# Two projections of a hybrid trunk layer by seven products in place of eight, and the last two groups of a third as one sum

## The chip, the cores and the metric

One core of a Trainium2 chip. The metric is device microseconds of one execution of the program; lower is better. The program holds two kernels one after the other: the fast one that is spoken of here, and a general one that runs only if the fast one, at its end, finds that some operand lay outside the range for which its number format holds.

## The reference

One layer for 1024 prompt tokens and 8 x 16 sample tokens (1152 columns in all), model width 1024:

```python
proj = h @ w_in                                   # q | k | v | SiLU gates | SSD x,B,C | dt | two merge gates
att_branch = (o_att.reshape(b, s, ATT_WIDTH) * jax.nn.silu(z_att)) @ w_att_proj    # 1024 -> 1024
...
y = rms_norm(y.reshape(b, s, SSD_GROUPS, SSD_WIDTH // SSD_GROUPS), ...)
ssd_branch = y.reshape(b, s, SSD_WIDTH) @ w_ssd_proj                               # 2048 -> 1024
merged = jax.nn.sigmoid(g_att) * att_branch + jax.nn.sigmoid(g_ssd) * ssd_branch
out = x + gate * (merged @ w_out)                                                  # 1024 -> 1024
```

The change touches the last three products: the attention projection, the SSD projection and the output projection.

## The kernel before

Activations lie transposed, 128 channels on the partitions and the 1152 tokens as columns. Every float32 operand of a large product is split into a float16 high part and a float16 low part, and a product is three matmuls: high x high, high x low, low x high (L709, L710, L712 in `dense`). The split of a tile is one ScalarE copy (the high part) and one VectorE instruction `x*scale - hi` (the low part): L627 and L628 in `halves` for weights, 1024 columns each, L1946 and L1948 in `split` for operands, 1152 columns each. `level` (L619) is a ScalarE square with a sum that records the mean size of what was split; `verdict` compares all of these with bounds at the end.

`dense` makes one tile of 128 output channels: for each of three groups of 384 tokens it sums over the 8 tiles of the operand, 3 matmuls each, in one PSUM bank (tag "d", three slots; "g" has three, "s" one of two banks). With `wide`, the three groups advance together, tile by tile, so that a first output tile can begin before the last operand tile is there.

The tail of the program is a row of stages on TensorE. First come the last of the gate products, which still use the 8 operand tiles of the input (`hops`). Then the attention projection, `att_dense`: 8 output tiles; each group's bank is read by one VectorE instruction that multiplies it with a gate tile (L1998). Then the SSD projection, `ssd_dense`, 4 groups of 4 operand tiles; for each group all 8 output tiles are made, and each bank is read by L2007 (times the gate) and added to the running sum by L2008. Then the output projection, `out_dense`, whose banks are read by L2070 (times the modulation, plus the residual), L2074 and L2076 for the samples, and stored. Beside these run the generators `att_prep` (loads the 8 attention tiles and starts their splits), `gate_loads`, `ssd_prep` (loads the SSD tiles, scales them by the norm, L1986, and starts their splits) and `mod_gate` (a small product for the modulation, within the attention projection).

The order of the instructions on each engine is not the order of the Python code: the class `Order` takes the recorded program, its dependencies and a table of costs, and lays every engine's instructions out by a list scheduler. Each engine then works through its own list strictly in that order, with semaphores between engines. Loads and stores of the tail are issued by SyncE's queue, in its own fixed order; among them are two short transfers, `ya` (L1133, stores three rows of token sums) and the load that brings them back (L1141), which belong to the norm of the last SSD group.

Of the kernel before, what the change touches and what calls it, by code (L numbers as in the profile page):

```python
# [64 lines left out]
X_MEAN = (0.25, 2.0 ** 19)  # L65

# [353 lines left out]
def trunk_kernel(ctx: ExitStack, tc: tile.TileContext, h, again):  # L420
# [42 lines left out]
    NPART, NOPER = 121, 48  # L463
    sums = fix(NPART + 2 + NOPER)
# [34 lines left out]
    L_TAIL = arena.set_layout(Z0, [("T", 15, NT)])  # L499
    L_SM = arena.set_layout(Z0 + 15 * NT, [("e", 2, 384)])  # L500
# [14 lines left out]
    def alloc(lay, tag, cols):  # L515
        if lay is L_H or lay is L_W or lay is L_W3 or lay is L_Q or lay is L_V:
            return Buf(arena, arena.alloc(lay, tag, cols // 2), cols, True)
# [83 lines left out]
    def job(*raw):  # L601
        jobs.append([len(parts) + i for i in range(len(raw))])
        parts.extend(raw)
# [9 lines left out]
    meant = {"w": 0, "x": NPART + 2}  # L613
# [15 lines left out]

    def w_split(i, keep=lambda x: x):  # L630

        n = len(jobs[i])
        w = parts[jobs[i][0]].shape[1]
        if i not in wsplit:
            lay = L_W3 if n > 1 else L_W
# [41 lines left out]
    def w_done(i):  # L677
        for x in wsplit.pop(i)[:2]:
            x.free()
# [10 lines left out]
    for x in [h["wall"][i] for i in range(29, 85)] + [h["watt"][i] for i in range(8)] + [h["wssd"][i] for i in range(16)] \  # L690
            + [h["wout"][i] for i in range(8)]:
        job(x)
# [1242 lines left out]
    gates = []  # L1935

# [5 lines left out]

    def split(t, ops, scale):
        hi = yield from walloc(L_H, "h", NT)
        lo = yield from walloc(L_H, "h", NT)
# [7 lines left out]

    att_ops, out_ops = [], []
    ssd_ops = [[] for _ in range(NG)]

    def att_prep():
        yield from ready(lambda: ssd_all[NPAIR])
        for u in range(NU):
            t = yield from walloc(L_TAIL, "T", NT)  # L1960
            dma(t.ap, att_d[u])
            yield from pause(3000)
            urgent.append(split(t, att_ops, SA))

    def gate_loads():
        yield from ready(lambda: len(att_ops) >= NU - 1)
        for i in range(16):
            t = yield from walloc(L_TAIL, "T", NT)
            dma(t.ap, gate_d[i])
            gates.append(t)  # L1970
            yield from pause(5000 if i < 2 else 10500)

    def ssd_prep(g):
        yield from ready(lambda: len(ssd_ops[g - 1]) == PPG if g else len(att_ops) == NU)
# [3 lines left out]
        for j in range(PPG + 1):  # L1978
# [5 lines left out]
            if j:  # L1984
# [4 lines left out]
                urgent.append(split(t, ssd_ops[g], SA))  # L1989

    def att_dense():
        for c in range(8):
            def ev(o, g, tok, ps, c=c):
                while len(gates) <= c:
                    blocked[0] = "gates"
                    yield None
                x = gates[c].ap[:, tok]
                nc.vector.scalar_tensor_tensor(x, x, 1.0, ps, ALU.add, ALU.mult)  # L1998
# [1968 lines left out]
```

## Time and profile before

| | us |
|---|---|
| median of 3 runs | 1764.83 (1762.36 to 1766.66) |
| the profiled execution | 1765.52 |
| its span | 1763.6 |
| TensorE busy | 1738.2 (99%) |
| VectorE busy | 1230.0 (70%) |
| ScalarE busy | 957.8 (54%) |
| GpSimd busy | 347.3 (20%) |
| granted TensorE clock, mean | 0.998 |

A matmul's duration in the profile is from its start until its result is out; matmuls overlap, so what counts is the time from one start to the next. Loads of weights ("PEld") are engine time of their own that overlaps the matmuls. Durations of VectorE and ScalarE include a small overlap with the next instruction.

### The profile page before, as it was taken

The numbers are of one execution on the slowest core, as the hardware profiler recorded it, in microseconds if no ns is written. First come the engines' busy times: TensorE is split into PE (matmuls) and PEld (weight loads), VectorE is DVE, ScalarE is ACT, GpSimd is POOL, SyncE is SP. The second block draws the span as 40 slices with busy tenths as digits, with TensorE's granted clock in tenths as the row PEclk, the third lists the DMA queues.
The fourth block names the chain that finished last, engine by engine and source line by source line (L and its number), as shares of the span: only waits on it lengthen the run. The fifth ranks groups of instructions, "written<-read, shape, count | busy, mean of one in ns | idle before, by whom it ended". The sixth has DMA issues, their size and how long they took to land.

```text
span 1763.6 us, 34941 instructions
## 1 busy us (share of the span) xinstructions
PE 1738.2 (99%) x13821; PEld 1092.9 (62%) x13821; DVE 1230.0 (70%) x2327; ACT 957.8 (54%) x1903; POOL 347.3 (20%) x624
## 2 busy tenths in 40 slices
PE   7999999999999999999999999999999999999998
PEld 3556556555556566666666666666666556666665
DVE  6458677877776967787878677777775526876732
ACT  8766555556465565656764656456552616342510
POOL 0233323323133011321312131112222100000000
PEclk9999999999999999999999999999999999999999
DMA  9248878988887584533554445435577734311321
GB/s 381 74 125 206 196 213 198 206 211 195 204 232 165 148 230 131 174 114 124 174 158 114 107 132 181 140 117 133 165 227 271 270 103 156 102 49 50 128 104 56
DMA packets 266565, 284.87 MB, mean 162 GB/s; under 512 B 199628, under 2 KB 200664, under 8 KB 266392
## 3 DMA queue, kind: packets, MB, share of 16 engines
q1 hardware_dynamic: 257432, 253.90, 51.9%
q0 software_dynamic: 8960, 28.65, 4.3%
q8 instruction: 110, 1.80, 0.4%
q14 instruction: 63, 0.52, 0.1%
HBM read 192.70 MB, written 43.66 MB: 134 GB/s over the span
## 4 chain that ended last, share of the span: by engine, by line
PE 87%; DVE 5%; ACT 4%; DMA 2%; issue 1%; POOL 1%; SPq 0%; DVEq 0%; POOLq 0%; ACTq 0%
PE d L709 19%; PE d L710 18%; PE d L712 18%; PE d L762 5%; PE d L764 5%; PE d L763 5%; PE g L1368 2%; PE s L1855 2%; PE g L1827 2%; PE g L1875 1%; PE s L1415 1%; PE g L1415 1%; PE g L712 1%; PE g L710 1%; PE g L709 1%
## 5 line engine op out<-in xcount | busy, mean ns | idle before, releaser
L709 PE MATMUL d<-arena 128*128 128x384 f16 x2172 | 709.6, 327 | 1.4 <-ACT arena L1543 1.4
L710 PE MATMUL d<-arena 128*128 128x384 f16 x2172 | 708.7, 326 | 0.0
L712 PE MATMUL d<-arena 128*128 128x384 f16 x2172 | 708.6, 326 | 0.0
L709 PEld LDWEIGHTS <-arena 128*128 128x128 f16 x2280 | 223.5, 98 | 147.8 <-issue 10.5
L712 PEld LDWEIGHTS <-arena 128*128 128x128 f16 x2280 | 223.2, 98 | 147.8 <-issue 0.5
L710 PEld LDWEIGHTS <-arena 128*128 128x128 f16 x2280 | 223.3, 98 | 138.0 <-issue 2.0
L619 ACT ACTIVATE arena<-arena 128x1024 bf16<-128x1024 f32 (+3 forms) x169 | 181.5, 1074 | 145.0 <-DMA arena<-in_wall_dram 82.4
L627 ACT ACTIVATE arena<-arena 128x1024 f16<-128x1024 f32 (+1 forms) x117 | 122.4, 1046 | 124.5 <-PE d L710 112.6
L762 PE MATMUL d<-arena 128*128 128x384 f16 (+1 forms) x568 | 186.8, 329 | 0.0
L764 PE MATMUL d<-arena 128*128 128x384 f16 (+1 forms) x568 | 186.1, 328 | 0.0
L763 PE MATMUL d<-arena 128*128 128x384 f16 (+1 forms) x568 | 186.1, 328 | 0.0
L628 DVE SCALAR_TENSOR_TENSOR arena<-arena 128x1024 f16<-128x1024 f32 (+1 forms) x117 | 145.3, 1246 | 42.3 <-ACT arena L627 41.7
L1308 ACT ACTIVATE arena<-arena 128x640 f32<-128x640 f32 (+4 forms) x144 | 100.8, 701 | 62.6 <-DVE arena L1311 62.1
L1566 DVE SCALAR_TENSOR_TENSOR arena<-arena 128x1176 f32<-128x1176 f32 x72 | 107.2, 1489 | 2.3 <-issue 0.9
L1754 ACT ACTIVATE arena<-arena 128x128 f32<-128x128 f32 x288 | 89.9, 390 | 28.0 <-DMA arena<-acs_d 26.3
L762 PEld LDWEIGHTS <-arena 128*128 128x128 f16 x576 | 56.3, 98 | 50.7 <-issue 17.5
L1344 DVE SCALAR_TENSOR_TENSOR arena<-arena 128x640 f16<-128x640 f32 (+4 forms) x128 | 86.9, 711 | 0.0
L1236 POOL TENSOR_SCALAR arena<-arena 128x16 f32<-128x16 f32 (+1 forms) x24 | 10.0, 415 | 356.3 <-DVE arena L1209 356.1
L764 PEld LDWEIGHTS <-arena 128*128 128x128 f16 x576 | 56.4, 98 | 38.4 <-issue 0.2
L1203 ACT ACTIVATE arena<-d 128x256 f32<-128x256 f32 x71 | 26.8, 378 | 96.1 <-PE d L764 96.1
L763 PEld LDWEIGHTS <-arena 128*128 128x128 f16 x576 | 56.4, 98 | 32.8
L1311 DVE CUSTOM_DVE_ANT_0 arena<-s,arena 128x320 f32<-128x320 f32 (+4 forms) x128 | 60.2, 502 | 19.4 <-PE s L1473 9.4
(242 smaller groups left out, 2596.4 us busy)
## 6 DMA issues: line engine op xcount, KB each, us to landing
arena<-in_wall_dram SPq DMA_DIRECT2D x85, 512.0 KB
arena<-acs_d SPq DMA_DIRECT2D x32, 576.0 KB
arena<-in_kc_dram SPq DMA_DIRECT2D x64, 256.0 KB
arena<-in_vc_dram SPq DMA_DIRECT2D x64, 256.0 KB
arena<-in_wada_dram SPq DMA_DIRECT2D x24, 512.0 KB
arena<-in_xT_dram SPq DMA_DIRECT2D x16, 576.0 KB
gate_d<-arena POOLq DMA_DIRECT2D x48, 192.0 KB, 4.0
arena<-eacs_d SPq DMA_DIRECT2D x32, 288.0 KB
```

What stands on the lines that cost most here:

```text
L619: keep(nc.scalar.activation(junk[:, :n], x, AF.Square, scale=scale * n ** -0.5, accum_out=sums[:, c:c + 1]))
L627: keep(nc.scalar.activation(hi, x, AF.Copy, scale=scale))
L628: keep(nc.vector.scalar_tensor_tensor(lo, x, scale, hi, ALU.mult, ALU.subtract))
L709: nc.tensor.matmul(ps, hi.r[:, wc], kh.r[:, tok], start=k == 0, stop=False)
L710: nc.tensor.matmul(ps, hi.r[:, wc], kl.r[:, tok], start=False, stop=False)
L712: nc.tensor.matmul(ps, lo.r[:, wc], kh.r[:, tok], start=False, stop=k == nk - 1)
L762: nc.tensor.matmul(ps, kh.r[:, tok], wh, start=k == 0, stop=False)
L763: nc.tensor.matmul(ps, kh.r[:, tok], wl, start=False, stop=False)
L764: nc.tensor.matmul(ps, kl.r[:, tok], wh, start=False, stop=k == KT - 1)
L1308: nc.scalar.activation(p, p, AF.Exp, bias=sm_[:, 4 + e:5 + e], scale=-1.0, accum_out=sm_[:, 6 + e:7 + e])
L1566: nc.vector.scalar_tensor_tensor(yc, r.ap[:, j:j + n], w4[:, i, j:j + 1], yc, ALU.mult, ALU.add)
L1754: nc.scalar.activation(me[e].ap[:, cs], me[e].ap[:, cs], AF.Relu, scale=-1.0, bias=a4[:, c, hds[e]:hds[e] + 1])
```

## The change

In `att_dense` and `out_dense`, two output tiles (256 channels) and the two halves of the tokens (576 each) form a 2 x 2 block product over pairs of operand tiles. The new `quad_dense` makes it by Strassen's scheme in Winograd's form: 7 products instead of 8, each over 4 pairs of operand tiles, in two banks of 288 tokens, 3 matmuls each. What the scheme adds:

- `quad_split` makes four sums of 512 columns of the two weight tiles and splits 3.5 tiles where 2 were split (each of 1024 columns).
- `pieces` takes two operand tiles, makes four sums of 576 columns, and splits 3.5 tiles of 1152 columns where 2 were split; `level` reads the four half tiles.
- `joined` (L795 of the changed kernel) adds a product's two banks to a running sum, seven times for each block product; the first product is copied out by ScalarE (L816; at the first block product of a stage a second one too, L820).

All of these sums are VectorE's. In `ssd_dense` groups 2 and 3 become one sum over 8 operand tiles, so that the banks are read for three groups, not for four. Sizes of pools, the loads' conditions and the bounds of `verdict` follow.

```diff
+    def quad_split(i):
...
+        a, b = ([x.ap.rearrange("p (k e m) -> p e k m", e=2, m=P)[:, e] for e in range(2)] for x in w)
...
+        halves(bufs[0].r, bufs[1].r, w[0].ap, SW)
+        nc.vector.tensor_tensor(t[0], b[0], b[1], ALU.add)
+        nc.vector.tensor_tensor(t[1], t[0], a[0], ALU.subtract)
+        nc.vector.tensor_tensor(t[2], a[0], b[0], ALU.subtract)
+        nc.vector.tensor_tensor(t[3], a[1], t[1], ALU.subtract)
...
+        halves(bufs[3].r, bufs[4].r, u[0].ap, SW)
+        halves(k4(bufs[2].r[:, :512]), k4(bufs[2].r[:, 512:]), b[1], SW)
+        halves(bufs[5].r, bufs[6].r, u[1].ap, SW)
...
+    HT = NT // 2
+    HC = NT // 4
+
+    def quad_dense(ops, evict, last=False, wide=False):
...
+        def product(q, banks, ks=range(4)):
...
+                for g, ps in enumerate(banks):
+                    c = slice(g * HC, (g + 1) * HC)
+                    nc.tensor.matmul(ps, wh, xh[:, c], start=k == 0, stop=False)
+                    nc.tensor.matmul(ps, wh, xl[:, c], start=False, stop=False)
+                    nc.tensor.matmul(ps, wl, xh[:, c], start=False, stop=k == 3)
...
+        def joined(t, banks, op):
+            y = yield from walloc(L_TAIL, "T", HT)
+            for g, ps in enumerate(banks):
+                c = slice(g * HC, (g + 1) * HC)
+                nc.vector.tensor_tensor(y.ap[:, c], t.ap[:, c], ps, op)
+            return y
+
+        def bank(n):
+            if n % 3 == 0:
+                x = pss.tile([P, 2, 512], F32, tag="s", name=nm("s"))
+                return [x[:, g, :HC] for g in range(2)]
+            if n % 3 == 1:
+                return [pg(HC) for _ in range(2)]
+            return [psd.tile([P, HC], F32, tag="d", name=nm("d")) for _ in range(2)]
...
+        if wide:
+            qs = (0, b), (1, bank(1)), (2, bank(2))
+            for k in range(4):
+                for q, x in qs:
+                    yield from product(q, x, (k,))
...
+        s1 = yield from walloc(L_TAIL, "T", HT)
+        for g, ps in enumerate(b):
+            nc.scalar.activation(s1.ap[:, g * HC:(g + 1) * HC], ps, AF.Copy)
...
+        yield from product(1, b)
+        c = yield from joined(s1, b, ALU.add)
+        yield from evict(0, 0, c) or ()
+        b = bank(2)
+        yield from product(5, b)
+        u2 = yield from joined(s1, b, ALU.add)
...
+        yield from product(6, b)
+        u3 = yield from joined(u2, b, ALU.add)
...
+        yield from product(4, b)
+        c = yield from joined(u3, b, ALU.add)
+        yield from evict(1, 1, c) or ()
+        u4 = yield from joined(u2, b, ALU.add)
...
+        yield from product(3, b)
+        c = yield from joined(u3, b, ALU.subtract)
+        yield from evict(1, 0, c) or ()
...
+            yield from product(2, b)
+        c = yield from joined(u4, b, ALU.add)
+        yield from evict(0, 1, c) or ()
...
+    def pieces(ta, tb, ops, scale):
...
+        got[0], = yield from halved(b11, HT)
+        got[1], got[2] = yield from halved(tb.ap[:, :NT], NT)
...
+        nc.vector.tensor_tensor(t1, b12, b11, ALU.subtract)
+        nc.vector.tensor_tensor(t2, b22, t1, ALU.subtract)
+        nc.vector.tensor_tensor(t3, b22, b12, ALU.subtract)
+        nc.vector.tensor_tensor(t4, t2, b21, ALU.subtract)
+        for x in (b11, b12, b21, b22):
+            level(x, scale, kind="h")
...
+        got[4], got[5] = yield from halved(u[0].ap[:, :NT], NT)
+        got[6], got[3] = yield from halved(u[1].ap[:, :NT], NT)
...
     def ssd_dense(g):
...
-            yield from dense(ssd_ops[g], ev, nk=4, outs=2, last=cp == 3, other=g < NG - 1)
+            yield from dense(ssd_ops[g], ev, nk=4 if g < NL else 8, outs=2, last=cp == 3, other=g < NL)
...
     def out_dense():
...
+            def ev(o, t, y, c=c, xs=xs):
...
+                nc.vector.scalar_tensor_tensor(x.ap[:, a:a + n], y.ap[:, :n], m[:, 0:1], x.ap[:, a:a + n], ALU.mult, ALU.add)
+                if t:
...
+                    nc.vector.tensor_tensor(y3, y3, m[:, 1:].unsqueeze(2).to_broadcast([P, NB, NS]), ALU.mult)
+                    nc.vector.tensor_tensor(x.ap[:, NP:], x.ap[:, NP:], y.ap[:, n:], ALU.add)
+                dma(h["out_y"][c + o][:, a:a + HT], x.ap[:, a:a + HT])
```

Since the scheduler lays the engines' lists out anew, three places are shown. The first is SyncE's queue around the token sums of the last SSD group, shortly before the attention projection. `att_d` is the attention's result, `ya` the row of sums. Before:

```order
L1981 DMA arena_73<-y_d_76 128x1152
L1969 DMA arena_73<-gate_d_79 128x1152
L2026 DMA arena_73<-in_wada2_dram 128x1024
L1981 DMA arena_73<-y_d_76 128x1152
L2026 DMA arena_73<-in_wada2_dram 128x1024
L609 DMA arena_73<-in_watt_dram 128x1024
L1969 DMA arena_73<-gate_d_79 128x1152
L1133 DMA ya692_15201<-arena_73 1x384 x3
L1969 DMA arena_73<-gate_d_79 128x1152
L1141 DMA arena_73<-ya692_15201 128x9
```

Now:

```order
L2204 DMA arena_73<-att_d_75 128x1152
L618 DMA arena_73<-in_watt_dram 128x1024
L2214 DMA arena_73<-gate_d_79 128x1152
L1296 DMA ya692_15231<-arena_73 1x384 x3
L2214 DMA arena_73<-gate_d_79 128x1152
L2276 DMA arena_73<-in_wada2_dram 128x1024
L1304 DMA arena_73<-ya692_15231 128x9
L2204 DMA arena_73<-att_d_75 128x1152
L2276 DMA arena_73<-in_wada2_dram 128x1024
```

Before, all eight loads of `att_d` stood ahead of `ya` (the last of them ahead of the rows shown); now the eighth stands behind both transfers of the token sums (L1296 and L1304 are the old L1133 and L1141).

The second is ScalarE's list at the entry of the attention projection. L1658 (now L1821) is the tanh that empties a bank of the last gate product. Before, L1946 is the high part of an operand and L619 a `level`:

```order
L1658 ACTIVATE arena<-d_15185 128x384
L619 ACTIVATE arena<-arena 128x1152
L1946 ACTIVATE arena<-arena 128x1152
L1658 ACTIVATE arena<-d_15186 128x384
L1658 ACTIVATE arena<-d_15187 128x384
L1946 ACTIVATE arena<-arena 128x1152
L619 ACTIVATE arena<-arena 128x1152 x3
L627 ACTIVATE arena<-arena 128x1024
```

Now L2165 is a high part in `pieces`, L628 a `level`, L636 a high part of weights, L816 and L820 the copies out of PSUM:

```order
L1821 ACTIVATE arena<-d_15215 128x384
L1821 ACTIVATE arena<-d_15216 128x384
L1821 ACTIVATE arena<-d_15217 128x384
L2165 ACTIVATE arena<-arena 128x576
L628 ACTIVATE arena<-arena 128x576 x4
L2165 ACTIVATE arena<-arena 128x1152 x2
L628 ACTIVATE arena<-arena 128x1024 x2
L816 ACTIVATE arena<-s_15353 128x288 x2
L636 ACTIVATE arena<-arena 128x1024
L820 ACTIVATE arena<-d_15356 128x288
L820 ACTIVATE arena<-d_15357 128x288
```

Behind the last tanh stood one high part of an operand; now three high parts and six `level`s stand between it and the four copies that empty banks.

The third is VectorE's list at the end of the program. Before, the last two banks are read by one instruction each:

```order
L2055 TENSOR_SCALAR arena_73<-g841_18278 128x48
L2076 TENSOR_TENSOR arena_73<-arena_73 128x128
L2056 SCALAR_TENSOR_TENSOR arena_73<-arena_73 128x48
L2057 TENSOR_REDUCE arena_73<-arena_73 128x1
L2060 TENSOR_SCALAR again_58<-g842_18285 1x1
L2070 SCALAR_TENSOR_TENSOR arena_73<-d843_18289,arena_73 128x384
L2070 SCALAR_TENSOR_TENSOR arena_73<-d844_18316,arena_73 128x384
```

Now (L2333, L2336 and L2337 are the old L2070, L2074 and L2076; L2319 is the old L2060):

```order
L795 TENSOR_TENSOR arena_73<-arena_73,d861_18717 128x288
L2316 TENSOR_REDUCE arena_73<-arena_73 128x1
L2333 SCALAR_TENSOR_TENSOR arena_73<-arena_73 128x576
L795 TENSOR_TENSOR arena_73<-arena_73,s862_18746 128x288
L2319 TENSOR_SCALAR again_58<-g859_18711 1x1
L795 TENSOR_TENSOR arena_73<-arena_73,s862_18746 128x288
L2333 SCALAR_TENSOR_TENSOR arena_73<-arena_73 128x448
L2336 TENSOR_TENSOR arena_73<-arena_73 128x128
L2337 TENSOR_TENSOR arena_73<-arena_73 128x128
```

Behind the last product stood one instruction; now six stand there, and the verdict's last step is among them.

More of the change, by code (lines that the diff above doesn't have):

```diff
@@ L677, in w_done @@
     def w_done(i):
-        for x in wsplit.pop(i)[:2]:
+        w = wsplit.pop(i)
+        for x in w[0] if i in quads else w[:2]:
             x.free()
@@ L1935, in trunk_kernel @@
     gates = []
+    gone = [0]
     def gates_dense():
@@ L1988, in ssd_prep, with ev @@
                     rb.free()
[L1989 removed]
+                urgent.append(split(t, ssd_ops[min(g, NL)], SA))
     def att_dense():
[L1992 to L1994 removed]
+        for c in range(0, 8, 2):
+            def ev(o, t, y, c=c):
+                while len(gates) <= c + o:
                     blocked[0] = "gates"
                     yield None
[L1997 to L2000 removed]
+                x = gates[c + o].ap[:, t * HT:(t + 1) * HT]
+                nc.vector.scalar_tensor_tensor(x, x, 1.0, y.ap, ALU.add, ALU.mult)
+                y.free()
+            yield from quad_dense(att_ops, ev, last=c == 6, wide=c == 0)
+            gone[0] = c + 2
     def ssd_dense(g):
```

262 lines of the change are left out of this document (211 added, 51 removed).

## The prediction

> **What bounds the kernel now.** First the page's head and the engines' totals:
>
> ```profile
> span 1763.6 us, 34941 instructions
> ...
> PE 1738.2 (99%) x13821; PEld 1092.9 (62%) x13821; DVE 1230.0 (70%) x2327; ACT 957.8 (54%) x1903; POOL 347.3 (20%) x624
> ```
>
> TensorE is busy 99% of the span, VectorE 70%. Then the tail by stages: the gate products, the attention projection, the SSD projection, the output projection, and what lies behind the last matmul (columns: TensorE, weight loads, VectorE, ScalarE, GpSimd busy, granted clock, DMA share, GB/s).
>
> ```profile
> 1310.00:1376.00 66.00, 66.00 (x471) 42.68 (x469) 36.44 (x49) 23.56 (x36) 17.70 (x26) 1.00 0.76 267
> 1376.00:1475.00 99.00, 99.00 (x626) 58.68 (x624) 39.01 (x52) 37.74 (x57) 4.61 (x12) 1.00 0.48 174
> 1475.00:1663.00 188.00, 188.00 (x1159) 113.20 (x1158) 147.72 (x231) 75.52 (x101) 0.00 (x0) 1.00 0.28 89
> 1663.00:1757.40 94.40, 94.30 (x582) 56.58 (x580) 32.28 (x62) 21.51 (x31) 0.00 (x0) 1.00 0.27 96
> 1757.40:1763.60 6.20, 0.00 (x0) 0.00 (x0) 0.56 (x1) 0.00 (x0) 0.00 (x0) 0.77 0.12 40
> ```
>
> TensorE never waits there. So a matmul taken from these stages is worth its pitch, as long as VectorE and ScalarE empty the banks in time. VectorE is used 39 of 99 us in the attention projection and 32 of 94 in the output projection, so that the added sums fall where it has room; in the SSD projection it works 148 of 188 us and TensorE still loses nothing.
>
> **The matmuls.** The pitch is read from starts, here of the last gate product; between the first and the last row lie 23 matmuls:
>
> ```profile
> 1374.22 0.33 PE L712 MATMUL d<-arena 128*128 128x384 f16 x1
> ...
> 1377.96 0.33 PE L710 MATMUL g<-arena 128*128 128x384 f16 x1
> ```
>
> 3.74/23 = 0.1626 us for 384 columns. Removed are 2 projections x 8 tiles x 8 operand tiles x 3 groups x 3 = 1152 of these, 187.3 us. Added are 8 block products x 7 x 4 x 2 banks x 3 = 1344 of 288 columns. None of that width is in the trace, so I bound it by neighbours: 416 columns in a dense product, and two widths of the attention scores, with the matmul behind each.
>
> ```profile
> 548.02 0.35 PE L762 MATMUL d<-arena 128*128 128x416 f16 x1
> ...
> 548.91 0.34 PE L764 MATMUL d<-arena 128*128 128x416 f16 x1
> 364.85 0.67 PE L1415 MATMUL s<-arena 64*128 64x128 f16 x12
> 365.45 0.34 PE L762 MATMUL d<-arena 128*128 128x384 f16 x1
> 370.65 0.82 PE L1415 MATMUL s<-arena 64*128 64x512 f16 x6
> 371.40 0.34 PE L762 MATMUL d<-arena 128*128 128x384 f16 x1
> L709 PEld LDWEIGHTS <-arena 128*128 128x128 f16 x2280 | 223.5, 98 | 147.8 <-issue 10.5
> ```
>
> 416 columns: 0.89/5 = 0.178, so in proportion to 384 (0.176) within the rounding of the starts; a line through 384 and 416 would give 0.116 at 288, a saving of 30.9 us, the far end below. The scores (half arrays, 128 columns in 0.60/12 = 0.050, 512 in 0.75/6 = 0.125) have a fixed part of 0.025; with that at full array 288 columns would be 0.025 + 0.1376 x 0.75 = 0.128, a saving of 187.3 - 172.3 = 15.0, the far end above. I take the proportion, 0.122, since 416 against 384 is the same form of matmul: 163.9 us, a saving of **23.4**. A weight load (98 ns) still fits beside 122.
>
> The Trainium skill (TensorE: Matmul & The Clock Gate, "Wait — 56ns, not 53.3ns?") speaks against this a little: warm matmuls start N/2.4 GHz plus a fixed 2.5 ns apart, and this change issues 192 more. By it 288 columns are 122.5 ns, and the saving 22.7 us in place of 23.4; the rows at 384 and 416 fit it as well as the proportion.
>
> **VectorE.** The durations:
>
> ```profile
> L628 DVE SCALAR_TENSOR_TENSOR arena<-arena 128x1024 f16<-128x1024 f32 x36 | 44.4, 1233 | 12.0 <-ACT arena L627 11.9
> L1948 DVE SCALAR_TENSOR_TENSOR arena<-arena 128x1152 f16<-128x1152 f32 x32 | 43.1, 1353 | 16.5 <-ACT arena L1946 16.3
> L1986 DVE SCALAR_TENSOR_TENSOR arena<-arena 128x1152 f32<-128x1152 f32 x16 | 22.6, 1415 | 9.4 <-DMA arena<-y_d 6.8 <-DMA arena<-yb 2.5
> L1621 DVE TENSOR_TENSOR arena<-g,arena 128x288 f32<-128x288 f32 x1 | 0.4, 440 | 0.0
> L1881 DVE TENSOR_TENSOR arena<-arena 128x512 f32<-128x512 f32 x16 | 11.0, 690 | 0.4
> L2007 DVE SCALAR_TENSOR_TENSOR arena<-arena,d 128x384 f32<-128x384 f32 x87 | 47.5, 550 | 25.5 <-PE d L712 25.5
> L2008 DVE TENSOR_TENSOR arena<-arena 128x384 f32<-128x384 f32 x96 | 52.2, 554 | 1.7
> ```
>
> For one block product: 14 joins x 0.44 = 6.2; 4 evictions of 576 columns at 0.76 (between 0.55 at 384 and 1.23 at 1024) = 3.0; the next weights 2 x 1.23 + 0.69 for 512 = 3.2 and four sums x 0.69 = 2.8. Together 15.2 us beside 168 x 0.122 = 20.5 of TensorE. The attention projection adds the first SSD operands (5 x 1.415 + 4 x 1.353), the first SSD weights and small things: 73 us beside 82 plus 5 of the modulation's matmuls, 84%. The output projection has about 70 beside 82. The operands of each projection cost 4 pairs x (0.76 + 3 x 1.35 + 4 x 0.76) = 31 us where 8 x 1.35 = 11 stood; for attention this lies beside the gate products (36 of 66 us used), for the output beside the SSD sum over 8 tiles, which in turn loses 24 x (0.550 + 0.554) = 26.5 us of bank reading. That fusion takes no matmul away and TensorE did not wait there, so it is worth **0** by itself, but it is the cover of the rest: the SSD stage then has 148 - 26.5 + 31 + 6 (the first output weights) = 158 us of VectorE work in 188, and without it 185, 98%.
>
> TensorE is ahead of VectorE by two products at most: the banks go s, g, d in turn, and a product lasts 2.9 us. I walked the second block product of the attention projection, with the modulation in it, through the new order: each bank was emptied before it was needed, by 0.5 us or more. A wait of 0.25 us at each of the 56 products would be 14 us, the far end; none is the near one, to which the walk is nearer. I take **1.0**.
>
> **The entry of the attention projection.** The rows on the eighth load and ScalarE:
>
> ```profile
> 1365.80 0.85 PE L1128 MATMUL g<-arena 128*32 128x384 f32 x6
> 1367.21 0.84 SPq L1133 DMA_DIRECT2D ya<-arena  x3
> 1370.37 0.34 SPq L1141 DMA_DIRECT2D arena<-ya  x1
> 1376.82 0.33 PE L709 MATMUL g<-arena 128*128 128x384 f16 x1
> y_d<-arena POOLq DMA_DIRECT2D x16, 576.0 KB, 4.5
> L1946 ACT ACTIVATE arena<-arena 128x1152 f16<-128x1152 f32 x32 | 36.0, 1152 | 34.1 <-PE g L712 16.3 <-DVE arena L2008 10.3 <-PE d L712 7.4
> L627 ACT ACTIVATE arena<-arena 128x1024 f16<-128x1024 f32 x113 | 118.9, 1052 | 124.5 <-PE d L710 112.6 <-PE g L710 11.6
> L619 ACT ACTIVATION_READ_ACCUMULATOR arena<-arena 128x1 f32 x169 | 32.0, 189 | 0.0
> L1614 ACT ACTIVATE arena<-g 128x288 f32<-128x288 f32 x1 | 0.4, 410 | 3.3 <-PE g L1613 3.3
> ```
>
> Call the projection's first matmul T (1376.82). The load behind L1141 goes out at T-6.0 and, by the 4.5 us that a transfer of this size takes, lands at T-1.5. What needs it late is the fourth pair: TensorE has 54 matmuls (6.6 us) before it. VectorE makes the three sums, the low part and the rest by about T+8.7, product 5 wants its piece at T+9.9. ScalarE is tighter: after the last tanh (T+0.7) come 0.65 (576 columns, between 0.41 at 288 and 1.15 at 1152), four `level`s (3.4, with 0.19 each for the read-out), two high parts (2.3), two `level`s of weights (2.5), so that the copies of the first bank end at T+10.3 and, after 1.05 and 0.41, the first of the other at T+11.8. TensorE wants these at T+10.2 and T+11.1: a stall of **1.0**, between 0 (pitches are some 0.1 under the durations) and 4.5 (one more landing).
>
> At the output projection the same walk from the last three SSD banks (six readings, three sums, two splits: about T+6.2 for the first pieces, wanted at T+6.6) gives nothing.
>
> **The end.**
>
> ```profile
> 1756.97 0.33 PE L712 MATMUL d<-arena 128*128 128x384 f16 x1
> 1757.34 0.62 DVE L2070 SCALAR_TENSOR_TENSOR arena<-d,arena 128x384 f32<-128x384 f32 x1 [3.28 <-PE d L712]
> 1757.98 0.33 SPq L2081 DMA_DIRECT2D out_y_dram<-arena  x1
> L2076 DVE TENSOR_TENSOR arena<-arena 128x128 f32<-128x128 f32 x8 | 2.3, 292 | 0.2
> ```
>
> One reading of 0.62 becomes 2 x 0.44, the verdict's last step (at most the 0.29 of 128 columns), 0.68 for 448 columns and 2 x 0.29: 2.4 us, all on the path; the last store is 288 KB, not 192. I take **+1.8**; the ends are 1.0 (the first bank read early) and 3.5 (the store held up by the register load, which now stands just ahead of it on SyncE).
>
> **Sum.** 1763.6 - 23.4 + 1.0 + 1.0 + 1.8 = 1744.0 for the span. The median lies 1.2 above this span (the profiled execution 1.9), so the forecast is **1745.2**.
>
> **Rivals.**
>
> VectorE becomes the bound. It works its list strictly in order, and behind each join stand weights and operands of the next block. If through such waits it gets only 75% of a stage, the projections last 73/0.75 = 97 and 70/0.75 = 94 us in place of 87 and 82: +22, so 1767; at 70% it is +35 and 1781. The gain is gone when the 56 products lose 0.35 us each. For it speaks the 84%; against it the SSD stage, 79% with TensorE at 188 of 188.
>
> The handovers are dearer: the eighth load lands 4.5 us later and the output's first pieces 3 us later, +7, so 1752. For it: the load's place behind two short transfers; against: 6.6 us of cover.
>
> The narrow matmul has the scores' fixed part: a saving of 15, so 1754. Against it stand the 416 columns.
>
> The change does not do what it says: the new bounds of the verdict fail, the general kernel runs too, and the time is beyond 3400 (at least the 1738 us of matmuls again). The halves' squares are compared within a factor of 64; the inputs make the cached values of the samples 7.56 times larger, in 128 of the 576 tokens of one half: (448 + 128 x 57)/576, a factor of some 13.
>
> **How the numbers follow.** The forecast (1741 to 1749) 0.62; dear handovers (1749 to 1758) 0.16; the fixed part 0.05; VectorE as the bound 0.16, of which 0.06 within 0.2% (3.5 us, about what a measurement of this kernel can tell from no change) and 0.10 above; the general kernel 0.01. So faster 0.83, same 0.06, slower 0.11. The range 1740 to 1758 holds the forecast, the fixed part and the dear handovers, 0.83; what it leaves out is VectorE as the bound and the general kernel.
>
> **What would show it.** Starts of 288-column matmuls 0.122 apart, and the span from the first of them in a projection to its last about 82 us (87 with the modulation); a wrong pitch shows there and nowhere else. TensorE's idle time by releaser: ScalarE, L820, about 1 us at the first block product; VectorE, L795, near 0. From the last matmul to the last store 2.4 us where 1.0 stood. VectorE near 84% in both projections with TensorE full. Idle TensorE in front of many products, released by L795, would make the forecast wrong, and idle time at the fourth pair's matmuls would make the handover the reason.

## The result, and the profile after

The changed kernel takes 1750.38 us, median of four executions (1747.50 to 1752.57), against 1765.39 of the kernel before (1762.36 to 1766.66): a ratio of 0.9916, 95% interval 0.9897 to 0.9936. The forecast was 1745.2. In the profiled executions the span fell from 1763.6 to 1748.3 us, by 15.3 where 19.6 were forecast. The page's head and totals of the changed kernel:

```profile
span 1748.3 us, 35611 instructions
...
PE 1718.8 (98%) x14013; PEld 1113.4 (64%) x14013; DVE 1312.6 (75%) x2477; ACT 995.8 (57%) x1987; POOL 351.4 (20%) x624
```

The missing 4.3 us are lost in one stage. The changed kernel's stages, cut at the first matmul of each (attention projection, SSD projection, output projection, the end; columns as in the prediction):

```profile
1376.10:1470.40 94.30, 91.43 (x722) 69.87 (x720) 68.67 (x117) 40.12 (x65) 8.55 (x13) 0.96 0.51 168
1470.40:1657.60 187.20, 187.20 (x1154) 112.73 (x1153) 150.04 (x218) 88.57 (x130) 0.00 (x0) 1.00 0.33 115
1657.60:1740.20 82.60, 82.60 (x676) 65.85 (x673) 62.07 (x127) 24.11 (x39) 0.00 (x0) 1.00 0.33 115
1740.20:1748.30 8.10, 0.20 (x3) 0.09 (x2) 2.05 (x6) 0.00 (x0) 0.00 (x0) 0.66 0.19 69
```

The SSD projection (187.2) and the output projection (82.6 of the forecast 82) run full. The attention projection took 94.3 where 87 were forecast, with TensorE idle for 2.9 us and a mean granted clock of 0.96. What TensorE waited for in the tail (us in total, times, longest):

```profile
PE g L1010 <- ACT arena L2283: 2.5, 1, 2.5
PE d L781 <- ACT arena L820: 0.3, 1, 0.3
```

L820 is the entry of the projection, as forecast. L1010 is not in the forecast: it is the second step of the modulation (`mod_sum`, eight small matmuls), and it waits for ScalarE's copy of the first step's result. TensorE's timeline around it (start, duration, idle time ahead and its releaser):

```profile
1391.49 1.92 PE L1004 MATMUL g<-arena 128*32 128x512 f32 x16
...
1395.44 0.29 PE L783 MATMUL g<-arena 128*128 128x288 f16 x1
1398.24 1.88 PE L1010 MATMUL g<-arena 128*128 128x9 f32 x8 [2.52 <-ACT arena L2283]
1399.97 0.40 PE L781 MATMUL g<-arena 128*128 128x288 f16 x1
1400.16 0.45 PE L782 MATMUL g<-arena 128*128 128x288 f16 x1
...
1404.72 0.35 PE L783 MATMUL d<-arena 128*128 128x288 f16 x1
1404.90 0.29 PE L781 MATMUL d<-arena 128*128 128x288 f16 x1
```

Behind the idle 2.5 us the matmuls start 0.24 us apart in place of 0.122, until 1404.8. The windows show the granted clock (third column from the end) in the same stretch:

```profile
1396.00:1398.00 2.00, 0.00 (x0) 0.00 (x0) 1.96 (x4) 1.97 (x5) 0.00 (x0) 1.00 0.00 0
1398.00:1400.00 2.00, 1.76 (x9) 1.76 (x10) 1.38 (x2) 1.40 (x3) 0.00 (x0) 0.50 0.44 111
...
1404.00:1406.00 2.00, 2.00 (x14) 1.49 (x13) 1.62 (x5) 0.00 (x0) 0.00 (x0) 0.79 0.94 357
```

So the wait cost 2.52 us, then some 20 matmuls at 0.240 in place of 0.122 (2.35 us), and eight small ones in 1.73 in place of some 0.9 (0.85): **5.7 us**. The Trainium skill (TensorE: Matmul & The Clock Gate, "What's actually happening") has the clock fall to half after an idle window of about 3.4 us, counted freely; here 2.5 us of idleness were enough (the last section has more on it). How the copy came to be late is read upward, on ScalarE, on VectorE and on SyncE's queue:

```profile
1387.27 0.71 ACT L820 ACTIVATE arena<-d 128x288 f32<-128x288 f32 x2
1394.08 1.16 ACT L2141 ACTIVATE arena<-arena 128x1152 f16<-128x1152 f32 x1 [6.10 <-DVE arena L2231]
...
1397.61 0.58 ACT L2283 ACTIVATE arena<-g 128x512 f32<-128x512 f32 x1
```

```profile
1392.62 1.42 DVE L2231 SCALAR_TENSOR_TENSOR arena<-arena 128x1152 f32<-128x1152 f32 x1 [3.35 <-DMA arena<-yb]
```

```profile
1385.59 0.32 SPq L1308 DMA_DIRECT2D yb<-arena  x1
1385.96 1.41 SPq L2276 DMA_DIRECT2D arena<-in_wada_dram  x1
1387.47 0.38 SPq L2221 DMA_DIRECT2D arena<-yb  x1
```

```profile
SPq L2221 <- DVE arena L2243: 0.3, 1, 0.3
```

L2141, the high part of the first SSD operand, stands ahead of the copy L2283 in ScalarE's list, though TensorE does not need it for over 70 us more. It waits for L2231, the scaling by the norm, and this for the load L2221 of the norm's row. That load goes out at 1387.47: it stands behind the store L1308 in SyncE's queue (1385.59), and its buffer comes free last, with VectorE's L2243 (the last row, of SyncE's waits). It lands some 5 us later. In the kernel before, the same load had been issued at 1335.9 (first view), ScalarE made the copy right behind the modulation's first matmuls, and the second ones came 13 us after it (second view, third view):

```profile
L1976 SPq DMA_DIRECT2D arena<-yb x4: 319/320/320, 1335.9 to 1490.9; - x4
```

```profile
1391.44 0.57 ACT L2033 ACTIVATE arena<-g 128x512 f32<-128x512 f32 x1
```

```profile
1404.76 0.82 PE L847 MATMUL g<-arena 128*128 128x9 f32 x6
```

### The profile page after: what moved, and what is told of

Same layout as the page of the kernel before. It is cut to its first block, busy times and chain, and to the rows that moved or that the text cites. A ratio compares the mean times of both kernels' runs of the same rounds, so it can differ in the third digit from the quotient of the medians.

```text
span 1748.3 us, 35611 instructions
## 1 busy us (share of the span) xinstructions
PE 1718.8 (98%) x14013; PEld 1113.4 (64%) x14013; DVE 1312.6 (75%) x2477; ACT 995.8 (57%) x1987; POOL 351.4 (20%) x624
## 4 chain that ended last, share of the span: by engine, by line
PE 87%; ACT 4%; DVE 4%; DMA 2%; issue 1%; POOL 1%; SPq 0%; DVEq 0%; ACTq 0%; POOLq 0%
PE d L872 16%; PE d L873 16%; PE d L875 16%; PE d L925 5%; PE d L927 5%; PE d L926 5%; PE g L1531 2%; PE s L2018 2%; PE g L1990 2%; PE g L2038 1%; PE s L783 1%; PE s L781 1%; PE s L782 1%; PE s L1578 1%; PE g L1578 1%
## 5 line engine op out<-in xcount | busy, mean ns | idle before, releaser
L872 PE MATMUL d<-arena 128*128 128x384 f16 x1872 | 611.8, 327 | 1.4 <-ACT arena L1706 1.4
L873 PE MATMUL d<-arena 128*128 128x384 f16 x1872 | 610.7, 326 | 0.0
L875 PE MATMUL d<-arena 128*128 128x384 f16 x1872 | 610.7, 326 | 0.0
L875 PEld LDWEIGHTS <-arena 128*128 128x128 f16 x1896 | 185.7, 98 | 122.9 <-issue 0.5
L872 PEld LDWEIGHTS <-arena 128*128 128x128 f16 x1896 | 185.7, 98 | 121.5 <-issue 8.6
L873 PEld LDWEIGHTS <-arena 128*128 128x128 f16 x1896 | 185.7, 98 | 113.5 <-issue 2.0
L628 ACT ACTIVATE arena<-arena 128x1024 bf16<-128x1024 f32 (+4 forms) x185 | 184.6, 998 | 106.1 <-DMA arena<-in_wall_dram 65.4
L637 DVE SCALAR_TENSOR_TENSOR arena<-arena 128x1024 f16<-128x1024 f32 (+2 forms) x133 | 160.0, 1209 | 35.1 <-ACT arena L636 33.3
L636 ACT ACTIVATE arena<-arena 128x1024 f16<-128x1024 f32 (+2 forms) x133 | 135.5, 1021 | 85.3 <-PE d L873 15.5
L925 PEld LDWEIGHTS <-arena 128*128 128x128 f16 x576 | 56.3, 98 | 50.8 <-issue 17.5
L927 PEld LDWEIGHTS <-arena 128*128 128x128 f16 x576 | 56.4, 98 | 38.4 <-issue 0.2
L926 PEld LDWEIGHTS <-arena 128*128 128x128 f16 x576 | 56.4, 98 | 32.8
```

Of the source, the lines that this page charges most:

```text
L628: keep(nc.scalar.activation(junk[:, :n], x, AF.Square, scale=scale * n ** -0.5, accum_out=sums[:, c:c + 1]))
L636: keep(nc.scalar.activation(hi, x, AF.Copy, scale=scale))
L637: keep(nc.vector.scalar_tensor_tensor(lo, x, scale, hi, ALU.mult, ALU.subtract))
L872: nc.tensor.matmul(ps, hi.r[:, wc], kh.r[:, tok], start=k == 0, stop=False)
L873: nc.tensor.matmul(ps, hi.r[:, wc], kl.r[:, tok], start=False, stop=False)
L875: nc.tensor.matmul(ps, lo.r[:, wc], kh.r[:, tok], start=False, stop=k == nk - 1)
```

## The experiments

**The late operand.** The scaling of the first SSD operand is tied behind the first modulation in the program's order:

```diff
             if j:
                 p, t = g * PPG + j - 1, ts[j - 1]
+                if g == 0 and j == 1:
+                    yield from ready(lambda: len(modded) > 0)
-                late(nc.vector.scalar_tensor_tensor(t.ap, t.ap, par["ssd_g"][:, p:p + 1], rb.ap, ALU.mult, ALU.mult))
+                x = late(nc.vector.scalar_tensor_tensor(t.ap, t.ap, par["ssd_g"][:, p:p + 1], rb.ap, ALU.mult, ALU.mult))
+                if g == 0 and j == 1:
+                    pinned.add(x.ins.name)
...
             mod_bias(p2, js, free)
+            modded.append(i)
```

> The first SSD operand is made after the first modulation instead of ahead of it, on VectorE and so on ScalarE; nothing else is edited. Theory: what the change lost against the forecast is one wait in the attention projection, where the modulation's second matmuls wait 2.5 us for ScalarE's copy (which stands behind an SSD operand that waits for a late load), and the half clock after it (20 matmuls at 0.240 in place of 0.122 us, 2.35 us, and the eight small matmuls at 1.73 in place of 0.9). Without the wait all three go: 2.5 + 2.35 + 0.85 = 5.7 us less, a span of about 1742.6 and a time near 1744.7; the granted clock between 1392 and 1430 us is 1.00. Rival: the wait only hides the next late thing (the later SSD operands, VectorE with four of them in a shorter stretch), which then takes its place: time within 2 us of 1750.4, with a new idle row of TensorE in the attention or at the start of the SSD projection.

Measured: 1744.86 us (1743.97 to 1745.75), ratio 0.9887 (0.9872 to 0.9903). TensorE's timeline and the windows of the same place:

```profile
1391.29 1.92 PE L1004 MATMUL g<-arena 128*32 128x512 f32 x16
1395.36 0.95 PE L1010 MATMUL g<-arena 128*128 128x9 f32 x8
```

```profile
1392.00:1400.00 8.00, 8.00 (x70) 5.80 (x63) 6.54 (x15) 2.60 (x3) 0.00 (x0) 1.00 0.81 278
1400.00:1430.00 30.00, 30.00 (x250) 22.92 (x248) 27.98 (x48) 12.77 (x18) 0.00 (x0) 1.00 0.71 226
```

No idle time, clock 1.00, and nothing takes the wait's place: the attention projection lasts from 1375.97 to the first SSD matmul at 1464.26, 88.3 us. The 6.0 us between 94.3 and 88.3 are the difference of the two spans (1748.3 and 1742.2) but for 0.1. The theory holds.

**The changed kernel again**, to see whether the wait and the half clock are always there.

> The changed kernel once more, on the chip of the next two runs. Theory (the wait at the modulation's second matmuls is in the order of the lists, the length of the half clock behind it is not): the same idle row of 2.5 us (2.3 to 2.7), and half clock behind it for some 3 us (as without the fusion) or 6.7 us (as in the first profile), so 1747.5 to 1750.5 us. Rival (the first profile was an odd execution): no idle row there, or none with a lower clock.

Measured: 1748.77 (1745.48 to 1751.48), ratio 0.9902 (0.9887 to 0.9918). The idle row is the same, the half clock shorter:

```profile
1401.19 1.06 PE L1010 MATMUL g<-arena 128*128 128x9 f32 x8 [2.52 <-ACT arena L2283]
...
1402.34 0.29 PE L783 MATMUL g<-arena 128*128 128x288 f16 x1
1402.46 0.41 PE L781 MATMUL g<-arena 128*128 128x288 f16 x1
...
1405.79 0.34 PE L783 MATMUL d<-arena 128*128 128x288 f16 x1
1405.97 0.29 PE L781 MATMUL d<-arena 128*128 128x288 f16 x1
```

The half clock begins 1.3 us after work has resumed and lasts 3.4 us: about 1.65 us lost, where the first profile lost 3.2. Nine executions of this kernel lie between 1745.5 and 1752.6, four of the late operand's between 1744.0 and 1745.8. The changing length of the half clock fits that spread, and so do the mean clocks on record (0.997 and 0.998 in the three fastest of the nine, 0.995 to 0.997 in the others), but only two executions were profiled.

**Work in the wait.** Extra matmuls, whose results are overwritten, ahead of the modulation's second step; first behind its first step (20 of them), then directly ahead of its second (16):

```diff
-            ps, p2 = pg(), pg(36)
+            ps, p2 = pg(), pg()
             mod_cols(ps, ws, 512)
+            if i == 0:
+                f = att_ops[0][0][0]
+                for _ in range(20):
+                    pinned.add(nc.tensor.matmul(p2[:, :HC], f[:, :P], f[:, :HC], start=True, stop=True).ins.name)
```

> 20 matmuls of 288 columns whose results are overwritten (20 x 0.122 = 2.45 us) stand behind the first modulation's matmuls, so that TensorE works through the 2.5 us in which it otherwise waits; the chain of loads, VectorE and ScalarE that makes it wait is the same. Theory (idle time lowered the clock): the wait itself stays, as work of no use, but the clock stays at 1.00 and 2.35 + 0.85 = 3.2 us are saved: about 1747.2. Rival (the clock fell for another reason, such as the slow modulation matmuls, or its loss is counted twice with the wait): the half clock is there again and the time stays at 1750.4; if the wait had been no loss at all, the 20 matmuls would cost 2.45 us, 1752.8.

> The changed kernel with 16 matmuls of 288 columns (results overwritten, 16 x 0.122 = 1.96 us) directly ahead of the modulation's second matmuls, where TensorE waits; three more block matmuls stand ahead of them, so that of the 2.5 us about 0.2 stay idle. The chain of loads that makes it wait is the same. Theory (idle time lowers the clock): the wait costs its 2.5 us still (less 0.37 for the three matmuls), the granted clock stays at 1.00, and what the half clock cost goes: 2.35 + 0.85 us at most, so 1746.8 (to 1748.5, since in some runs of the changed kernel the half clock was shorter). Rival (the clock does not hang on the idle time): half clock again, 1750.0.

Measured: 1749.22 (1746.50 to 1750.53) and 1748.27 (1747.46 to 1748.61). Neither filled the wait as meant. In the first the extra work held a bank and moved the wait to the next product's bank, 1.66 us; in the second it waited itself, since its bank came free with the copy:

```profile
PE g L2293 <- ACT arena L2283: 1.5, 1, 1.5
PE s L781 <- ACT arena L816: 1.1, 1, 1.1
```

```profile
1396.00:1398.00 2.00, 0.47 (x4) 0.23 (x3) 1.90 (x5) 1.80 (x5) 0.00 (x0) 1.00 0.00 0
1398.00:1400.00 2.00, 2.00 (x19) 1.65 (x17) 1.93 (x4) 1.57 (x2) 0.00 (x0) 1.00 0.67 184
```

What they do show: with 1.66 and 1.53 us of idleness at this place the granted clock stayed at 1.00 in every window (above, of the second), where 2.5 us had brought it to 0.50. Whether work without use would keep the clock up is not shown, since neither run filled the wait. In the second, 1.53 idle and 1.96 of useless work stand where 2.52 and 3.2 stood, 2.2 us less. The times alone do not decide it: its median lies 2.1 under the changed kernel's first set of executions and 0.5 under the second.

**The fusion.** First undone with the seven products kept; then alone, with both projections as before the change; then undone with the late operand.

```diff
-    for i in range(8):
-        job(h["wssd"][i])
-    for i in range(8, 12):
-        job(h["wssd"][i], h["wssd"][i + 4])
+    for i in range(16):
+        job(h["wssd"][i])
...
-    NL = NG - 2
+    NL = NG - 1
...
-            yield from dense(ssd_ops[g], ev, nk=4 if g < NL else 8, outs=2, last=cp == 3, other=g < NL)
+            yield from dense(ssd_ops[g], ev, nk=4, outs=2, last=cp == 3, other=g < NL)
```

> Both projections keep the seven products, but the SSD projection is four sums over 4 tiles again. Theory of the prediction (the fusion is worth nothing by itself and is cover for the output's operands): VectorE is at 98% of the SSD stage, its work comes late at the output projection, and the time is 2 to 6 us above the changed kernel's, 1752 to 1756, with TensorE idle in the SSD stage or at the first output products, released by VectorE. Rival 1 (the cover is not needed): within 1 us of 1750.4. Rival 2 (at 98% strict order lets it fall behind): 15 us or more above.

> The last two SSD groups are one sum over 8 tiles; both projections are three groups of 384 columns as before the change. Theory (no matmul is taken away and TensorE waited for nothing there): the time of the kernel before, 1765.4 within 1.5 us. Rival (bank readings had cost TensorE something): up to 5 us less. A wait of the modulation's matmuls of some us, if the planner puts ScalarE's copy behind an SSD operand here too, would add up to 6 us and would show as an idle row of TensorE at the modulation with a lower clock behind it.

> The late operand, with the SSD projection as four sums over 4 tiles; seven products in both projections. Theory (the fusion is cover for the output's operands and first weights): the three waits on VectorE seen without the fusion, 1.35 + 0.82 + 1.45 = 3.6 us at the end of the SSD stage and the entry of the output projection, stay, and nothing else: 1744.9 + 3.6 = 1748.5. Rival (without the wait in the attention projection VectorE's work of the SSD stage is done earlier, so that no cover is needed): 1745.5 or less.

Measured: not fused 1753.41 (1752.63 to 1754.66); fused alone 1767.41, ratio 1.0012 (1.0003 to 1.0021); not fused with the late operand 1749.51 (1747.36 to 1753.46), so 4.6 above the late operand alone (ratios 0.9914 and 0.9887). What TensorE waits for in the last of these, beside the entry of its attention projection, where it waits 1.1 us longer than the late operand's kernel:

```profile
PE g L780 <- DVE arena L2165: 1.5, 1, 1.5
PE d L870 <- DVE arena L2256: 1.4, 1, 1.4
...
PE d L779 <- DVE arena L2256: 0.8, 1, 0.8
```

L2256 reads SSD banks, L2165 makes the low parts of the output's operands. Its windows around the hand-over:

```profile
1650.00:1660.00 10.00, 8.56 (x61) 5.75 (x59) 10.00 (x15) 4.86 (x8) 0.00 (x0) 1.00 0.41 150
1660.00:1670.00 10.00, 7.72 (x63) 5.89 (x62) 9.87 (x15) 7.97 (x16) 0.00 (x0) 1.00 0.19 59
```

VectorE works 19.9 of these 20 us. So the fusion is worth some 3.6 us as cover (1.45 + 1.35 + 0.82), and gains nothing alone: 2.2 us are lost, more than the 1.5 that the expectation allowed. The profile of the fusion alone has one wait of 0.9 us at the modulation's second step, where ScalarE's copy again stands behind an SSD operand. Where the rest of the 2.2 lies is open, since that profile (span 1763.3) is of the fastest of its executions.

**One projection at a time**, the other in three groups of 384 columns, both with the late operand and the fusion:

```diff
-        job(h["wout"][i], h["wout"][i + 1], quad=True)
+        job(h["wout"][i])
```

and the operands and evictions of that projection as before the change.

> Seven products in the attention projection only (with the late operand); the output projection in three groups of 384 columns as before, the fusion kept. Theory: half of the saving by pitch, 576 x 0.1626 - 672 x 0.1224 = 11.4 us, less 0.35 at the entry: 1765.2 - 11.0 = 1754.2. Rival (the attention projection gives less, as the operands' work beside the gate products and the SSD operands collide): 1756 to 1758.

> Seven products in the output projection only (with the late operand, since ScalarE's copy stood behind an SSD operand in the fused kernel too); the attention projection in three groups of 384 columns. Theory: 11.4 us saved, 1.7 lost at the end: 1765.2 - 9.7 = 1755.5. Rival (the joins of the output projection are late by 0.1 us or more a product, 28 products): 1758 or more. The two alone should add up to what both give: 11.0 + 9.7 = 20.7, against 1765.2 - 1744.9 = 20.3.

Measured: attention alone 1754.82, 11.0 us under the kernel before in the same set of runs (1765.81); output alone 1755.92, 9.9 under it. Each term is what was worked out, within intervals of some 2.4 us either way, and they add: 20.9 against 20.3 of both.

**VectorE's room.** Every join twice, on the late operand's kernel:

```diff
-                nc.vector.tensor_tensor(y.ap[:, c], t.ap[:, c], ps, op)
+                for _ in range(2):
+                    nc.vector.tensor_tensor(y.ap[:, c], t.ap[:, c], ps, op)
```

> The kernel of the late operand (1744.9), with every join of a product's bank on VectorE done twice (the same sum written again): 14 x 0.42 = 5.9 us more for a block product, 23.5 for a projection. Theory (VectorE has room for 16% and no more, and what goes beyond falls on TensorE one for one): attention 73 + 23.5 = 96.5 beside 87, output 70 + 23.5 = 93.5 beside 82, so 9.5 + 11.5 = 21 us more: 1766. Rival 1 (strict order: every product waits for its longer join, 56 products by 0.84 us): 47 us more, 1792. Rival 2 (the banks run far enough ahead, and VectorE's work of the projections spreads into the SSD stage): less than 8 us more, 1753 or under.

Measured: 1771.25 (1769.21 to 1776.48), ratio 1.0030 (1.0021 to 1.0040): 26 us above the late operand, nearer the theory's 21 than 47 or 8. Its three stages (the profile is of its slowest execution, in which the attention projection began 4.5 us later than with the late operand):

```profile
1380.50:1484.40 103.90, 93.35 (x722) 69.64 (x720) 88.52 (x167) 40.53 (x65) 8.56 (x13) 0.95 0.47 156
1484.40:1677.50 193.10, 189.10 (x1154) 113.27 (x1153) 153.95 (x225) 88.52 (x130) 0.00 (x0) 0.99 0.33 110
1677.50:1762.60 85.10, 82.99 (x676) 65.84 (x673) 80.34 (x175) 23.89 (x39) 0.00 (x0) 1.00 0.31 110
```

The sum was near, its parts were not. The attention projection takes 103.9 us where 88.3 stood, and the SSD projection 5.9 more, since its first weights are late (4.0 us of it in one wait for L637). The output projection bears the same joins for 2.6 (85.1 for 82.5), with VectorE at 80.3 of 85.1 us, but ends with VectorE behind: from the start of the last matmul (1762.30) to the end of the span stand 12.0 us, where the late operand's kernel has 8.4. In the attention projection VectorE is at 88.5 of 103.9, 85%, TensorE is idle for 10.6, and half clock behind two of the waits costs some 4.5 more. The longest waits are for a join (L796, 2.4 and 1.6) and for a high part of weights (L636, 4.0), so there the strict order makes VectorE the bound well before 100%, as the rival of the prediction had it, at a load that the change does not reach.

**The end shortened.** The last product's banks one after the other, the one with the samples first; then also the range decision one quadrant earlier:

```diff
+        if tail:
+            b = bank(1)
+            y = yield from walloc(L_TAIL, "T", HT)
+            for g in (1, 0):
+                yield from product(2, b, gs=(g,))
+                c = slice(g * HC, (g + 1) * HC)
+                nc.vector.tensor_tensor(y.ap[:, c], u4.ap[:, c], b[g], ALU.add)
+                evict(0, 1, y, g)
...
-                if c == 6 and (o, t) == (1, 1):
+                if c == 6 and (o, t) == (0, 0):
```

> The late operand, and in the output projection's very last product the second bank's matmuls first: its join, evictions and store (160 columns of the prompt, the samples) lie beside the first bank's 12 matmuls, and only one join (0.44), one step of 288 columns (0.55) and a store of 288 columns stand behind the last matmul, in place of 2.4 us. Theory (the end is that chain): from the last matmul's start to the end 6.9 us where 8.3 stood, 1743.5. Rival (the last store's way out sets the end, and it is the number of stores that counts): no change, 1744.9.

> As the short end, with the small products and reductions of the data-range decision (the flag read at the end) issued at the last block's first quadrant in place of its second, so that TensorE does not wait 0.98 us for VectorE's reduction ahead of the last 24 matmuls. Theory: that idle second goes, the end stays at 6.8 us from the last matmul's start: 1.6 us under the late operand's kernel, 1743.3. Rival: the decision's steps now delay VectorE's joins in the middle of the block, and what is won is lost there: 1744.9 or more, with idle rows released by VectorE's joins behind the first quadrant.

Measured: 1744.88 (1742.53 to 1749.47), ratio 0.9895, and 1744.70 (1744.30 to 1745.45), ratio 0.9878 (0.9862 to 0.9895). In the profile of the second, the last matmul starts at 1735.98 and the span ends at 1742.6: 6.6 us, where 8.4 stood with the late operand (1733.83 to 1742.2). The end is that chain, but its 1.8 us are within what these intervals can tell, and the time is not shown to be lower than 1744.86: in the profile of the second TensorE also waits 1.3 us longer at the entry of the attention projection, and 2.5 us near 1100 us, far ahead of the change. In the first, TensorE waited 1.0 us for the decision's reduction. Two of its five executions took 1748.7 and 1749.5, at a mean granted clock of 0.997 against 0.999; the difference is 3.5 us of lost clock, as much as two more stretches of 3.4 us at half clock would cost, but where they lay is open. The late operand (1744.0 to 1745.8) and this last kernel (1744.3 to 1745.5) are both faster than the changed kernel, of whose nine executions one, at 1745.5, lies as low.

## Why the prediction was right, and where it was not

**The pitch.** Right, and the largest term. The first and the 55th matmul of the attention projection:

```profile
1376.14 0.29 PE L781 MATMUL s<-arena 128*128 128x288 f16 x1
...
1382.75 0.29 PE L781 MATMUL s<-arena 128*128 128x288 f16 x1
```

6.61/54 = 0.1224 us, so the saving is 187.3 - 164.5 = 22.8 us, not 23.4, and the rival that took over the fixed part of the scores (0.128 us) is refuted. The Trainium skill (TensorE: Matmul & The Clock Gate, "Wait — 56ns, not 53.3ns?") gives 122.5 ns for 288 columns, with its fixed 2.5 ns; the trace agrees, 122.4 ns, where proportion gives 122.0.

**The banks.** 1.0 us was taken for 56 products; TensorE nowhere waits for L795. VectorE was over-estimated: 68.7 us in the attention projection (73 forecast), 62.1 in the output projection (70), 150 in the SSD projection (158). Single durations were added, while instructions that follow each other overlap: two splits of weights take 2.35 us together, not 2.46, two joins 0.82, not 0.88.

**The entry.** 1.0 forecast, 0.35 measured. It was 0.35 in four of the other kernels with seven products there, and 0.65 (the changed kernel again) to 1.65 where the copies L816 are late as well. The reason given holds: it is ScalarE's list, whose first copy L820 was forecast for T+11.8 and ended at about T+11.5. The load was read less well: the eighth went out at T-3.2 and landed at T+1.6, 3 us later than forecast, and the cover of 6.6 us was enough.

**The end.** +1.8 forecast. From the last matmul's start to the end of the span 8.3 us stand (1739.99 to 1748.3) where 6.6 stood: +1.7. The first and the last of VectorE's steps behind the last matmul, 2.1 us in all:

```profile
1740.32 0.46 DVE L795 TENSOR_TENSOR arena<-arena,s 128x288 f32<-128x288 f32 x1 [1.32 <-PE s L783]
...
1742.14 0.29 DVE L2337 TENSOR_TENSOR arena<-arena 128x128 f32<-128x128 f32 x1
```

**The fusion.** That the fusion is worth nothing by itself but is the cover of the rest held: 3.6 us of waits appear without it. The 98% without it was too high as a mean (with the late operand and without the fusion VectorE works 169 of the 194 us before the output projection, 87%), but the load is not spread evenly, and at the hand-over it is 100%.

**What failed** is the sentence "I walked the second block product of the attention projection, with the modulation in it, through the new order: each bank was emptied before it was needed". The banks were; the modulation's own hand-over was not walked. TensorE's second step needs a ScalarE copy, which stands behind an operand that needs VectorE, which waits for a load at the end of a queue. The rival of dear hand-overs had the right kind and size (+7, 1752), but named the eighth load and the output's first pieces; the load that was late is that of the norm's row. Of the 5.7 us, 2.5 are the wait; the rest is the clock behind it, for which the sum had no term. So 1750.38 lies inside the range of 1740 to 1758 through a rival whose places were others, and outside the 1741 to 1749 of the forecast itself: that the range held is in part luck. With the wait taken away the time is 1744.86, beside the forecast of 1745.2, but there errors cancel: the span of its profile is 1742.2 where 1744.0 was forecast (banks 1.0, entry 0.65 and an earlier start 0.85 less, pitch 0.6 more), and the median lies 2.7 above that span in place of 1.2.

The sum with what was measured: 1763.6 - 0.7 (the projection starts at 1376.14, not 1376.82) - 22.8 + 0.35 + 5.7 + 1.7 = 1747.9, beside 1748.3.

**VectorE as the bound** did not happen, at 73 and 75% where 84 and 85% were forecast (78% in the attention projection without the wait, 68.7 of 88.3 us). The doubled joins show how near it was. Of 23.5 us of added joins each, the output projection paid some 6, more than half of them behind its last matmul; the attention projection and what it makes for the SSD stage paid some 21, the half clock included.

## What to carry to other kernels

When engines work through fixed lists, follow every small product on the bounding engine back through the lists that feed it, not only the large ones: one operand made 70 us too early put 2.5 us of a load's delay on TensorE. Price an idle stretch of TensorE with the half clock that can follow it, which here cost 1.65 or 3.2 us behind 2.5. A part of a change that gains nothing alone can carry the rest, so take it away before calling it free.

## What the runs showed of the hardware

In the stages after 1376 us, idle times of 0.9, 1.5 and 1.7 us left the granted clock at 1.00. Those of 2.5 us, in three profiles, brought it to 0.50, for 3.4 us in two of them (the changed kernel again, and not fused) and for 6.8 us in the first; so did one of 2.4 and two of 4.0 us with the doubled joins. In the two it fell only after work had resumed, 1.2 to 1.3 us behind the idle time's end.

This is no threshold at 2.5 us. All these kernels, the one before too, have a wait of 2.0 to 2.5 us for GpSimd near 745 us, far ahead of the change. Behind 2.50 us of it the clock fell with the late operand (first two lines) and stayed at 1.00 with the short end (the other two), and in the kernel before 2.04 us were enough for half clock:

```profile
746.08 0.51 PE L2063 MATMUL g<-rarena 128*128 128x256 f32 x2 [2.50 <-POOL rarena L1979]
740.00:754.00 14.00, 11.15 (x58) 6.19 (x57) 12.34 (x12) 11.72 (x27) 6.88 (x9) 0.88 0.58 204
745.62 0.50 PE L2074 MATMUL g<-rarena 128*128 128x256 f32 x2 [2.50 <-POOL rarena L1990]
740.00:754.00 14.00, 11.50 (x72) 6.93 (x70) 11.88 (x11) 12.18 (x27) 6.88 (x9) 1.00 0.56 203
```

So what counts is also when the idle time falls. Away from the start and the end of the program each half clock lasted 3.41 or 6.83 us, and in the profiles with more than one the stretches between them are whole multiples of 3.413. In the changed kernel's profile these two windows hold the end of the early half clock and the start of the later one:

```profile
749.00:750.00 1.00, 1.00 (x6) 0.59 (x5) 1.00 (x2) 1.00 (x4) 0.25 (x1) 0.76 1.03 418
1397.50:1398.50 1.00, 0.26 (x2) 0.26 (x2) 0.90 (x2) 0.69 (x3) 0.00 (x0) 0.76 0.00 0
```

A mean of 0.76 over 1 us is half clock for 0.48 us, so the half clock ends at 749.48 and begins again at 1398.02: 648.54 us, 190 times 3.413. In the changed kernel again the same stretch is 651.94 us, 191 times. This fits a window of 3.413 us that runs freely, and is counted as idle when a large part of it, not all of it, is idle. How large a part is not settled. If the window's phase differs from one execution to the next, as the two outcomes of the same 2.50 us suggest, so does the price of the same wait.

At half clock the matmuls of 288 columns start 0.240 us apart. The Trainium skill (TensorE: Matmul & The Clock Gate, "Wait — 56ns, not 53.3ns?") states the columns divided by 1.2 GHz for the cold clock, with no fixed part, and the trace agrees: 240 ns.
